# Low parts and sums of squares on VectorE, and a block-wise store of h, in one stage of a hybrid decoder layer

## The chip, the cores and the metric

The kernel runs on one core of a Trainium2 chip. The metric is the device time of one execution in microseconds (us); the figure given is the median of several runs. The engines are called as in the profile: PE is TensorE (its weight loads are shown apart as PEld), DVE is VectorE, ACT is ScalarE, POOL is GpSimd, and SP is the engine whose queue issues nearly all DMA transfers. L702 means line 702 of the kernel before.

## The reference

One inference step of one decoder layer, for a prompt of 1024 tokens and 8 samples of 4 tokens each, 1056 tokens in all, with D = 1024:

```python
h = x + concat([rwkv7(z), pool(z)]) @ w_out        # z = rmsnorm(x) @ w_in
h = h + peer_ffn(rmsnorm(h))                       # product-key experts
h = h + (p @ ple_w) * sigmoid(rmsnorm(h) @ ple_gate_w)
y = rmsnorm(h)

# peer_ffn, for each token and each of 8 heads:
q = xn @ wq                                        # 8 heads x 2 halves x 128
s1, s2 = q[:, :, 0] @ keys[0].T, q[:, :, 1] @ keys[1].T
v1, i1 = top_k(s1, 16); v2, i2 = top_k(s2, 16)     # 128 keys each
sc, ci = top_k(v1[..., :, None] + v2[..., None, :], 16)
gate = softmax(sc)
out = sum_k gelu(u[expert_k] . xn) * gate_k * v[expert_k]
```

The results are the normed outputs and the new states of the recurrence and of the pooling. All of it is float32.

## The kernel before, in words

The hidden states are kept transposed: 128 features on the partitions, 8 blocks of features (KB = 8), and tokens along the free dimension. A product that needs float32 accuracy is made from three products in a faster rounded format (float32r): a matrix x is split into a high part hi, which is x rounded by ACT's copy, and a low part lo = x - hi, and the product is hi*hi + hi*lo + lo*hi (`mm3`, L647 to L656).

The program has these stages. `phase_a` makes the projections and the operands of the recurrence. `bchunk` works through the recurrence in chunks of 64 tokens (`b_stream`). `phase_c(gi)`, the function that the change edits, takes one group of tokens at a time; there are four groups (`GROUPS`): tokens 0 to 288, 288 to 544, 544 to 800 and 800 to 1056. `t_stream(gi)` selects the top experts of a group (`top`, `select`: many short DVE instructions) and writes the gates of the first 672 tokens as dense matrices, for which one-hot products on PE and copies on ACT are used (L901 to L912). The long last stage computes the experts densely for those 672 tokens on PE (L1112), while the remaining 384 tokens are served by gathered rows on POOL and DVE (L1221 to L1238), and then the last gate and norm.

`phase_c(gi)` does the following for its n = 288 or 256 tokens. It loads y, the output of the recurrence, and h, which already holds x and the pooling part of the first product. It splits the four blocks of y into `yhi` and `ylo` (`split`: ACT makes hi, POOL makes lo). For each of the 8 blocks b of h it loads the weights (`wblock`), makes the product (`mm3`), adds it to h (L696, DVE), squares the sum (L698, ACT) and adds the square to `sa` (L700, POOL). Then one DMA stores all 8 blocks of h to the DRAM tensor `hT_d` (L702), from which a later stage reads them. `sa` is summed over the partitions by a product with ones (L704), and `inv_sqrt` makes `rstd` from it (L178: square root on ACT; L179: reciprocal on DVE). L710 then scales each block of h in place on DVE, and `split` makes the high part (L679, ACT) and the low part of it (POOL). These are the operands of 16 more products with `wq`, whose results go through the keys (L739) to the score tensor `sc_d`, from which `top` of that group reads. The weights of groups 1 to 3 come from a stored split copy `wc_d` (L642 and L643, three buffers each); in group 0 they are split and stored on the way (L636 to L640).

The helper `PTT` (L126, L127) issues a tensor_tensor on POOL; `TT` issues one on DVE. In the profile all instructions of `PTT` stand on L127 and are told apart by their tiles: `lo<-y,hi`, `lo<-h,hi`, `sa<-sa,sq`.

What sets the order: `merge` interleaves the streams of one step as they are traced, in the proportion of their lengths. Step 1 runs `phase_c(0)` beside chunks of the recurrence, step 2 `phase_c(1)` beside the selection of group 0 and more chunks, step 3 `phase_c(2)` beside the selection of group 1, and step 4 `phase_c(3)` and the first 8 dense blocks (`upre`), with the selection of group 2 traced ahead of them. A planner then goes over the traced program with estimated costs and writes a fixed order for each engine (`schedule_with_timeline_sim=True`, L1403). On the chip each engine, and SP's queue of DMA issues, follows its written order; an instruction that waits holds back all that stands behind it. The planner also derives the waits from the reads and writes of tiles: L710, which overwrites h, waits for the store that reads it.

The lines that the change touches are L680, L700 and L702.

Of the kernel before, what the change touches and what calls it, by code (L numbers as in the profile page):

```python
# [10 lines left out]
F32 = mybir.dt.float32  # L11
# [5 lines left out]
ALU = mybir.AluOpType  # L17
# [46 lines left out]
def body(ctx, tc, io):  # L64
    nc = tc.nc
    mm = nc.tensor.matmul
    TT, STT, TS, ACT = (nc.vector.tensor_tensor, nc.vector.scalar_tensor_tensor, nc.vector.tensor_scalar,
                        nc.scalar.activation)
# [3 lines left out]
    hT_d = dram.tile([128, KB, T], F32, name="hT_d")  # L72
# [13 lines left out]
    def v3(ap, n):  # L86
        return ap.rearrange("p (a b) -> p a b", b=n)
# [5 lines left out]
    def vec(base, i):  # L93
        return vecs[:, base + i:base + i + 1]
# [31 lines left out]
    def PTT(out, a, b, op):  # L126
        nc.gpsimd.tensor_tensor(out, a, b, op=op)  # L127

    def PS(tag):
        return pools[tag].tile([128, 512], F32, name="ps", tag="bc" if tag in ("b0", "b1") else tag)  # L130
# [46 lines left out]
    def inv_sqrt(out, src, scale, eps):  # L177
        ACT(out, src, AF.Sqrt, bias=eps, scale=scale)  # L178
        nc.vector.reciprocal(out, out)  # L179
# [443 lines left out]
    def wblock(gi, b):  # L623
        if gi == 0 and b % 4 == 0 and b != 4:
            wraws[0] = gp.tile([128, EB, TC], F32, name="gst", bufs=2)
        if b >= C3E and gi == NG - 1:
            hi, lo = esplit(io["wq"][b - KB], PTT)
            return [(t[0], t[1]) for t in zip(*[(x[:, :HK], x[:, HK:]) for x in (hi, lo)])]
        out = []
        for i in range(1 if b < KB else 2):  # L630
            ks = slice(i * HK, (i + 1) * HK)
            hi = ws.tile([128, HK, 128], F32R, name="whi", bufs=3)
            lo = ws.tile([128, HK, 128], F32R, name="wlo", bufs=3)
            if gi == 0:
                raw = v3(wraws[0][:, 16 * (i + b % KB if b < KB else 2 * ((b - KB) % 4) + i):][:, :16].rearrange("p a b -> p (a b)"), 128)
                nc.sync.dma_start(raw, (io["w_out"][b] if b < KB else io["wq"][b - KB])[:, ks, :])  # L636
                ACT(hi, raw, AF.Copy)
                TT(lo, raw, hi.bitcast(F32), op=ALU.subtract)
                nc.sync.dma_start(wc_d[b, :, 0, ks, :], hi.bitcast(F32))
                nc.sync.dma_start(wc_d[b, :, 1, ks, :], lo.bitcast(F32))  # L640
            else:
                nc.sync.dma_start(hi.bitcast(F32), wc_d[b, :, 0, ks, :])  # L642
                nc.sync.dma_start(lo.bitcast(F32), wc_d[b, :, 1, ks, :])  # L643
            out.append((hi, lo))
        return out

    def mm3(ps, w, x, n):  # L647
        xhi, xlo = x
        K = len(w) * HK
        for k in range(K):  # L650
            whi, wlo = w[k // HK]
            kk = k % HK
            mm(ps[:, :n], whi[:, kk, :], xhi[:, k, :n], start=k == 0, stop=False)  # L653
            mm(ps[:, :n], whi[:, kk, :], xlo[:, k, :n], start=False, stop=False)  # L654
            l = mm(ps[:, :n], wlo[:, kk, :], xhi[:, k, :n], start=False, stop=k == K - 1)  # L655
        return l.ins  # L656
# [7 lines left out]
    def segs(gi):  # L664
        c0, c1 = GROUPS[gi]
        if c0 == 0:
            return ((0, NP, NSMP), (NSMP, 0, c1 - NSMP))
        return ((0, c0 - NSMP, c1 - c0),)

    def tiles_of(gi):  # L670
        n = GROUPS[gi][1] - GROUPS[gi][0]
        return [(t, min(128, n - t)) for t in range(0, n, 128)]

    def phase_c(gi):
        c0, c1 = GROUPS[gi]
        n = c1 - c0

        def split(k, src, hi, lo):
            ACT(hi[:, k, :n], src, AF.Copy)  # L679
            PTT(lo[:, k, :n], src, hi[:, k, :n].bitcast(F32), op=ALU.subtract)  # L680

        y = work.tile([128, 4, maxn], F32, name="y", tag="yp")
        nc.sync.dma_start(y[:, :, :n], y_d[:, :, c0:c1])
        h = work.tile([128, KB, maxn], F32, name="h")
        for d, s, L in segs(gi):
            nc.sync.dma_start(h[:, :, d:d + L], hx_d[:, :, s:s + L])
        yhi = mv.tile([128, KB, maxn], F32R, name="hi")
        ylo = mv.tile([128, KB, maxn], F32R, name="lo")
        for k in range(HK):
            split(k, y[:, k, :n], yhi, ylo)  # L690
        sa = work.tile([128, maxn], F32, name="sa")
        for b in range(KB):
            w = wblock(gi, b)
            ps = PS("b2")
            mm3(ps, w, (yhi, ylo), n)
            TT(h[:, b, :n], ps[:, :n], h[:, b, :n], op=ALU.add)  # L696
            sq = work.tile([128, maxn], F32, name="sq", bufs=1) if b else sa
            ACT(sq[:, :n], h[:, b, :n], AF.Square)  # L698
            if b:
                PTT(sa[:, :n], sa[:, :n], sq[:, :n], op=ALU.add)  # L700
            yield
        nc.sync.dma_start(hT_d[:, :, c0:c1], h[:, :, :n])  # L702
        psr = PS("b2")
        mm(psr[:, :n], ones, sa[:, :n], start=True, stop=True)  # L704
        rstd = work.tile([128, maxn], F32, name="rstd", tag="sa")
        inv_sqrt(rstd[:, :n], psr[:, :n], 1.0 / D, eps_t)
        nhi = mv.tile([128, KB, maxn], F32R, name="hi")
        nlo = mv.tile([128, KB, maxn], F32R, name="lo")
        for k in range(KB):
            STT(h[:, k, :n], h[:, k, :n], vec(V_G2, k), rstd[:, :n], op0=ALU.mult, op1=ALU.mult)  # L710
            split(k, h[:, k, :n], nhi, nlo)
        a, b = max(c0, GA), min(c1, GB)
        if a < b:
            for d, t in ((xh_d, nhi), (xl_d, nlo)):
                nc.sync.dma_start(d[:, :, a - GA:b - GA], t[:, :, a - c0:b - c0].bitcast(F32))
        for t0, m in tiles_of(gi):
            pos = c0 + t0
            if GA <= pos < GB:
                continue
            gp = pos - GB  # L720
            for half in range(2):
                ps = PS("b2")
                for k in range(4):
                    nc.tensor.transpose(ps[:m, k * 128:(k + 1) * 128], h[:, half * 4 + k, t0:t0 + m], ident)
                xt = work.tile([128, 512], F32, name="xt", tag="yp")
                ACT(xt[:m], ps[:m], AF.Copy)
                nc.sync.dma_start(xt_d[gp:gp + m, half * 512:half * 512 + 512], xt[:m])
        for j in range(HEADS // 2):
            q = work.tile([128, 4, maxn], F32, name="q", tag="yp")
            for i in range(4):  # L730
                w = wblock(gi, KB + 4 * j + i)
                ps = PS("b2")
                mm3(ps, w, (nhi, nlo), n)
                ACT(q[:, i, :n], ps[:, :n], AF.Copy)
                yield
            for t0, m in tiles_of(gi):
                ps = PS("b2")
                for i in range(4):
                    mm(ps[:m, i * 128:(i + 1) * 128], q[:, i, t0:t0 + m], keys[:, i % 2, :],  # L739
                       start=True, stop=True)  # L740
                st = tk.tile([128, 4, 128], F32, name="scs", bufs=2)
                ACT(st[:m], v3(ps[:m, :], 128), AF.Copy)
                nc.sync.dma_start(sc_d[TIDX[c0 + t0], :m, 4 * j:4 * j + 4, :], st[:m])
# [677 lines left out]
```

## Time and profile before

| | us |
|---|---|
| median of 3 runs | 3302.07 (3301.97 to 3302.18) |
| the profiled execution | 3310.19 |
| its span, first to last instruction | 3308.5 |
| PE busy | 3115.4 (94%) |
| DVE busy | 2561.4 (77%) |
| POOL busy | 1509.4 (46%) |
| ACT busy | 1127.6 (34%) |
| mean granted TensorE clock | 0.968 of full speed |

The profile shows one execution. Times inside it are counted from the first instruction of the span; the rest of the profiled execution's time, 1.7 us, lies around the span. A row of a timeline gives start, length, engine, line and operation, and in brackets how long the engine was idle before and what released it. A row of a group by line gives the shortest, median and longest duration in ns. An instruction's duration may overlap the next one's a little, so the busy time of a group can be less than count times mean.

### The profile page before, as it was taken

The numbers are of one execution on the slowest core, as the hardware profiler recorded it, in microseconds if no ns is written. First come the engines' busy times: TensorE is split into PE (matmuls) and PEld (weight loads), VectorE is DVE, ScalarE is ACT, GpSimd is POOL, SyncE is SP. The second block draws the span as 40 slices with busy tenths as digits, with TensorE's granted clock in tenths as the row PEclk, the third lists the DMA queues.
The fourth block names the chain that finished last, engine by engine and source line by source line (L and its number), as shares of the span: only waits on it lengthen the run. The fifth ranks groups of instructions, "written<-read, shape, count | busy, mean of one in ns | idle before, by whom it ended". The sixth has DMA issues, their size and how long they took to land.

```text
span 3308.5 us, 66279 instructions
## 1 busy us (share of the span) xinstructions
PE 3115.4 (94%) x26777; PEld 2995.7 (91%) x26777; DVE 2561.4 (77%) x4989; ACT 1127.6 (34%) x1734; POOL 1509.4 (46%) x1223
## 2 busy tenths in 40 slices
PE   8998898987888798999999999999999999999997
PEld 7886787877877787999999999999999999999996
DVE  7775333469689688888888888888888888888966
ACT  6442423434554555332222122122222222212243
POOL 5212232222132041146666665666566666666534
PEclk9999999998998898999999999999999999999998
DMA  3325557866875977569999999999999999999834
GB/s 117 117 88 126 156 139 231 277 177 179 241 218 179 296 237 229 198 225 343 336 345 337 327 348 331 327 344 344 330 334 347 331 329 341 337 327 343 316 109 129
DMA packets 437332, 858.88 MB, mean 260 GB/s; under 512 B 108960, under 2 KB 232096, under 8 KB 432544
## 3 DMA queue, kind: packets, MB, share of 16 engines
q1 hardware_dynamic: 326432, 451.93, 42.1%
q0 software_dynamic: 110592, 402.70, 33.6%
q8 instruction: 210, 3.44, 0.4%
q14 instruction: 98, 0.80, 0.1%
HBM read 733.92 MB, written 120.60 MB: 258 GB/s over the span
## 4 chain that ended last, share of the span: by engine, by line
PE 77%; DVE 9%; DMA 8%; ACT 2%; issue 2%; POOL 1%; SPq 1%; ACTq 0%; DVEq 0%; POOLq 0%
PE pd L1112 58%; PE ps L470 5%; PE ps L219 4%; PE ps L653 2%; PE ps L655 2%; PE ps L654 2%; DMA whi<-wc_d 2%; PE ps L909 2%; PE ps L302 1%; DMA scq<-sc_d 1%; DMA sc_d<-scs 1%; DMA wlo<-wc_d 1%; DMA hT_d<-h 1%; PE ps L739 1%; DVE I L762 1%
## 5 line engine op out<-in xcount | busy, mean ns | idle before, releaser
L1221 POOL DMA_INDIRECT row<-u,idx x384 | 546.6, 1423 | 313.8 <-DVE row L1229 134.1
L1221 POOL DMA_INDIRECT row<-v,idx x384 | 536.5, 1397 | 310.8 <-DVE po L1238 142.0
L1088 ACT ACTIVATE ehi<-eraw 128x1024 fp32r<-128x1024 f32 x278 | 294.7, 1060 | 1115.0 <-PE pd L1112 1014.7
L1112 PE MATMUL pd<-XH,elo 128*128 128x336 f32 x2176 | 514.7, 318 | 4.7 <-DVE elo L1090 3.1
L1112 PE MATMUL pd<-XL,ehi 128*128 128x336 f32 x2176 | 515.4, 318 | 0.0
L1112 PE MATMUL pd<-XH,ehi 128*128 128x336 f32 x2176 | 513.4, 317 | 0.3 <-ACT ehi L1088 0.2
L1112 PE MATMUL pd<-wh,ehi 128*128 128x336 f32 (+1 forms) x2112 | 503.4, 317 | 6.5 <-DVE tg L1302 6.5
L1112 PE MATMUL pd<-wh,elo 128*128 128x336 f32 (+1 forms) x2112 | 503.7, 317 | 0.0
L1112 PE MATMUL pd<-wl,ehi 128*128 128x336 f32 (+1 forms) x2112 | 502.3, 317 | 0.0
L1238 DVE SCALAR_TENSOR_TENSOR po<-row,act,po 128x1024 f32<-128x1024 f32 x381 | 488.6, 1283 | 6.7
L1229 DVE SCALAR_TENSOR_TENSOR row<-row,xt 128x1024 f32<-128x1024 f32 x384 | 455.7, 1220 | 9.7 <-DMA row<-u,idx 6.3
L1112 PEld LDWEIGHTS pd<-XH,elo 128*128 128x128 f32 x2176 | 374.1, 189 | 5.7 <-DVE elo L1090 3.5
L1090 DVE TENSOR_TENSOR elo<-eraw,ehi 128x1024 fp32r<-128x1024 f32 x256 | 315.8, 1234 | 79.0 <-ACT ehi L1088 73.2
L1112 PEld LDWEIGHTS pd<-XH,ehi 128*128 128x128 f32 x2176 | 373.3, 189 | 1.1 <-ACT ehi L1088 0.7
L1112 PEld LDWEIGHTS pd<-XL,ehi 128*128 128x128 f32 x2176 | 372.0, 189 | 0.2
L1112 PEld LDWEIGHTS pd<-wh,ehi 128*128 128x128 f32 x2112 | 362.3, 188 | 7.2 <-issue 7.0
L1112 PEld LDWEIGHTS pd<-wl,ehi 128*128 128x128 f32 x2112 | 362.4, 188 | 0.0
L1112 PEld LDWEIGHTS pd<-wh,elo 128*128 128x128 f32 x2112 | 361.7, 188 | 0.2
L653 PE MATMUL ps<-hi,whi 128*128 128x256 f32 (+1 forms) x592 | 189.3, 322 | 48.7 <-DMA whi<-wc_d 21.1
L127 POOL TENSOR_TENSOR ltm<-lts,nmt 128x256 f32<-128x256 f32 x98 | 82.1, 846 | 311.8 <-PE ps L470 189.0
L1181 DVE TENSOR_TENSOR OT<-pd,OT 128x672 f32<-128x672 f32 x120 | 102.9, 858 | 142.8 <-PE pd L1112 142.1
L910 ACT ACTIVATE gst<-ps 128x512 f32<-128x512 f32 x168 | 169.5, 1110 | 67.1 <-PE ps L909 62.0
(426 smaller groups left out, 5256.2 us busy)
## 6 DMA issues: line engine op xcount, KB each, us to landing
eraw<-uT SPq DMA_DIRECT2D x128, 512.0 KB, 6.4
eraw<-vP SPq DMA_DIRECT2D x128, 512.0 KB, 6.4
g_d<-gst SPq DMA_DIRECT2D x21, 2048.0 KB, 9.8
gq<-g_d SPq DMA_DIRECT2D x32, 1344.0 KB, 9.6
whi<-wc_d SPq DMA_DIRECT2D x108, 256.0 KB, 4.9
wlo<-wc_d SPq DMA_DIRECT2D x108, 256.0 KB, 5.2
fdc<-fd SPq DMA_DIRECT2D x16, 896.0 KB, 7.6
wc_d<-whi SPq DMA_DIRECT2D x40, 256.0 KB, 4.6
```

The source lines that it names most:

```text
L127: nc.gpsimd.tensor_tensor(out, a, b, op=op)
L219: mm(ps[:, :XW], s[:, k, :], x[:, k, a:b], start=first, stop=last)
L470: mm(o[hs], l[hs], r[hs], start=start, stop=stop)
L653: mm(ps[:, :n], whi[:, kk, :], xhi[:, k, :n], start=k == 0, stop=False)
L910: ACT(st[:, :, t2 + q:t2 + q + 4].rearrange("p e t -> p t e"), v3(ps, 128), AF.Copy, scale=1.0 / GS)
L1088: ACT(hi, raw, AF.Copy)
L1090: sub(lo, raw, hi.bitcast(F32), op=ALU.subtract)
L1112: mm(ps[:, a, :n], w_[:, k, :], x_[:, s:s + n], start=first, stop=last)
L1181: TT(halves(OT[db]), ps[:, :, :NH], halves(OT[db]), op=ALU.add)
L1221: nc.gpsimd.indirect_dma_start(out=r[:m], out_offset=None, in_=io[tab], in_offset=bass.IndirectOffsetOnAxis(ap=idx[:m, hh, k:k + 1], axis=0))
L1229: STT(r[:m], r[:m], 1.0, xt[:m], op0=ALU.mult, op1=ALU.mult, accum_out=pre[:m, k:k + 1])
L1238: STT(po[:m], r[:m], act[:m, k:k + 1], po[:m], op0=ALU.mult, op1=ALU.add)
```

## The change

In `phase_c`, the low part that `split` makes and the running sum of squares are issued on DVE (`TT`) instead of POOL (`PTT`). The store of h to `hT_d` is issued inside the loop over the blocks, one block at a time, behind the sum of that block's square, instead of once for all 8 blocks after the loop. Nothing else is edited; the values computed are the same.

```diff
         def split(k, src, hi, lo):
             ACT(hi[:, k, :n], src, AF.Copy)
-            PTT(lo[:, k, :n], src, hi[:, k, :n].bitcast(F32), op=ALU.subtract)
+            TT(lo[:, k, :n], src, hi[:, k, :n].bitcast(F32), op=ALU.subtract)
...
             ACT(sq[:, :n], h[:, b, :n], AF.Square)
             if b:
-                PTT(sa[:, :n], sa[:, :n], sq[:, :n], op=ALU.add)
-            yield
-        nc.sync.dma_start(hT_d[:, :, c0:c1], h[:, :, :n])
+                TT(sa[:, :n], sa[:, :n], sq[:, :n], op=ALU.add)
+            nc.sync.dma_start(hT_d[:, b, c0:c1], h[:, b, :n])
+            yield
```

## The prediction

> **What bounds the kernel now.** I read the busy shares and the slices first, then the chain of waits, then windows over the stretch that the edited function fills, then the timeline at the four places where a token group turns from its first product to its second. From the page, the busy row, the slices of PE and DVE, and the engines of the chain:
>
> ```profile
> PE 3115.4 (94%) x26777; PEld 2995.7 (91%) x26777; DVE 2561.4 (77%) x4989; ACT 1127.6 (34%) x1734; POOL 1509.4 (46%) x1223
> PE   8998898987888798999999999999999999999997
> DVE  7775333469689688888888888888888888888966
> PE 77%; DVE 9%; DMA 8%; ACT 2%; issue 2%; POOL 1%; SPq 1%; ACTq 0%; DVEq 0%; POOLq 0%
> ```
>
> A slice is 82.7 us. From the 17th slice on PE never leaves 9; before it PE has 7s and 8s. The windows (columns: length, then busy time of PE, PEld, DVE, ACT, POOL with counts, granted clock, DMA share, GB/s) split this at about 1345 us:
>
> ```profile
> 1345.00:3300.00 1955.00, 1938.67 (x12549) 1934.18 (x12548) 1672.57 (x2373) 520.42 (x639) 1163.82 (x826) 1.00 0.86 308
> 525.00:1340.00 815.00, 693.45 (x8950) 633.45 (x8948) 596.21 (x2235) 388.91 (x679) 192.54 (x233) 0.90 0.76 232
> 705.00:825.00 120.00, 93.52 (x1357) 83.76 (x1353) 113.23 (x542) 49.64 (x99) 36.75 (x52) 0.83 0.59 173
> 945.00:1060.00 115.00, 99.58 (x1456) 88.26 (x1454) 111.46 (x532) 52.52 (x104) 36.70 (x52) 0.87 0.64 191
> 1185.00:1245.00 60.00, 54.08 (x381) 51.93 (x380) 59.72 (x274) 31.83 (x49) 27.75 (x28) 0.94 0.68 209
> ```
>
> After 1345 us PE is busy 1938.7 of 1955 us and none of the edited lines runs there: that stage keeps its length. The change can act only on the 815 us before, where PE is idle 815 - 693.5 = 121.5 us. That is the most that could be won. The last three rows hold the turns of groups 1, 2 and 3. There DVE, which also runs the top-k selection of the group before, is busy 113.2 + 111.5 + 59.7 = 284.4 of 295 us (96%) while PE has 247.2 (84%). In the rest of the 815 us DVE has 311.8 of 520 (60%).
>
> **The turns.** Timeline rows (start, length, engine, line) of groups 0, 1, 2 and 3 in order:
>
> ```profile
> 564.05 0.46 DVE L696 TENSOR_TENSOR h<-ps,h 128x288 f32<-128x288 f32 x1 [0.83 <-PE ps L655]
> 565.62 6.60 SPq L702 DMA_DIRECT2D hT_d<-h  x1
> 567.29 1.95 DVE L179 RECIPROCAL rstd<-rstd 128x288 f32<-128x288 f32 x1 [2.18 <-ACT rstd L178]
> 577.75 2.35 DVE L710 SCALAR_TENSOR_TENSOR h<-h,vecs,rstd 128x288 f32<-128x288 f32 x4 [8.50 <-DMA hT_d<-h]
> 740.81 0.56 SPq L702 DMA_DIRECT2D hT_d<-h  x1
> 756.81 0.47 ACT L178 ACTIVATE rstd<-ps,eps_t 128x256 f32<-128x256 f32 x1
> 763.69 1.74 DVE L179 RECIPROCAL rstd<-rstd 128x256 f32<-128x256 f32 x1
> 767.05 5.63 DVE L710 SCALAR_TENSOR_TENSOR h<-h,vecs,rstd 128x256 f32<-128x256 f32 x8
> 982.64 1.75 DVE L179 RECIPROCAL rstd<-rstd 128x256 f32<-128x256 f32 x1
> 984.57 0.55 SPq L702 DMA_DIRECT2D hT_d<-h  x1
> 993.98 5.61 DVE L710 SCALAR_TENSOR_TENSOR h<-h,vecs,rstd 128x256 f32<-128x256 f32 x8 [2.00 <-DMA hT_d<-h]
> 1224.43 0.47 ACT L178 ACTIVATE rstd<-ps,eps_t 128x256 f32<-128x256 f32 x1
> 1228.52 1.73 DVE L179 RECIPROCAL rstd<-rstd 128x256 f32<-128x256 f32 x1
> 1231.95 5.61 DVE L710 SCALAR_TENSOR_TENSOR h<-h,vecs,rstd 128x256 f32<-128x256 f32 x8
> ```
>
> ```profile
> 566.00:579.00 13.00, 5.06 (x119) 4.44 (x120) 3.21 (x4) 2.18 (x5) 0.78 (x2) 0.84 0.92 242
> 735.00:768.00 33.00, 16.66 (x306) 14.08 (x301) 31.78 (x170) 6.66 (x17) 7.34 (x14) 0.71 0.38 101
> 975.00:996.00 21.00, 15.19 (x281) 12.87 (x279) 18.92 (x99) 10.98 (x25) 5.19 (x9) 0.81 0.79 221
> 1215.00:1234.00 19.00, 13.55 (x80) 12.25 (x78) 19.00 (x70) 9.76 (x17) 6.53 (x5) 0.90 0.61 200
> ```
>
> L710 overwrites h in place, so it has to wait until the one store of the whole h (L702) has read it. In group 0 rstd is ready at 569.24, and L710 starts at 577.75: 8.5 us that DVE spends idle on the store, and PE has only 5.06 of 13 us of work meanwhile. In group 2 rstd is ready at 984.39 and L710 starts at 993.98, with DVE filled by selection work for all but 2.0 us. In groups 1 and 3 no wait for the store shows, but the order on DVE and ACT, written beforehand by the planner, puts other work between: in group 3 rstd's square root ends at 1224.90, its reciprocal comes 3.6 us later. PE's idle time in the four rows is 7.9, 16.3, 5.8 and 5.5 us.
>
> **The change part by part.** The prices:
>
> ```profile
> L127 POOL TENSOR_TENSOR lo<-h,hi x32: 724/906/1179, 578.8 to 1238.8; 128x256 fp32r<-128x256 f32 x24, 128x288 fp32r<-128x288 f32 x8
> L127 POOL TENSOR_TENSOR lo<-y,hi x16: 722/738/1181, 522.9 to 1177.3; 128x256 fp32r<-128x256 f32 x12, 128x288 fp32r<-128x288 f32 x4
> L127 POOL TENSOR_TENSOR sa<-sa,sq x28: 716/740/1332, 541.5 to 1221.3; 128x256 f32<-128x256 f32 x21, 128x288 f32<-128x288 f32 x7
> L696 DVE TENSOR_TENSOR h<-ps,h x32: 398/416/459, 537.0 to 1220.3; 128x256 f32<-128x256 f32 x24, 128x288 f32<-128x288 f32 x8
> L710 DVE SCALAR_TENSOR_TENSOR h<-h,vecs,rstd x32: 458/944/1061, 577.7 to 1236.6; 128x256 f32<-128x256 f32 x24, 128x288 f32<-128x288 f32 x8
> L710 DVE SCALAR_TENSOR_TENSOR h<-h,vecs,rstd 128x256 f32<-128x256 f32 x24 | 16.8, 770 | 2.0 <-DMA hT_d<-h 2.0
> L638 DVE TENSOR_TENSOR wlo<-gst,whi x40: 668/691/1321, 528.3 to 678.1; 128x512 fp32r<-128x512 f32 x40
> ```
>
> *Stores by block.* The wait for one store of 1 MB becomes eight stores of 128 KB, seven of them long issued when rstd is ready. The last is read only by the eighth L710, some 3 us after the first. What is late next is rstd itself (569.24). Group 0: PE's 7.9 us of idle time go, and no other work is queued for DVE there; I take -8 (bounds 0 and -8.5). Groups 1 to 3: the planner no longer has to hold L710 behind the store, but the selection work that now fills DVE has to be done anyway; what PE can win is its idle time, 16.3 + 5.8 + 5.5 = 27.6 us at most, nothing at least. In group 1 the sequence waits behind selection on ACT and DVE as well, and the only store wait that DVE shows there is the 2.0 us of group 2. I take about a third: -10.
>
> *The queue on SP.* 28 DMA issues are added, none removed from the traffic: the same bytes in the same rows. A store of a similar kind and SP's waits:
>
> ```profile
> L1048 SPq DMA_DIRECT2D hx_d<-x x24: 319/327/3133, 421.7 to 516.0; - x24
> hx_d<-x SPq DMA_DIRECT2D x21, 176.0 KB, 2.3
> SPq L642 <- PE ps L655: 114.9, 46, 7.3
> PE ps L653 <- DMA whi<-wc_d: 21.1, 9, 4.9
> ```
>
> 28 x 0.33 = 9 us of SP's time over 815 us, on a queue that already waits 114.9 us for PE to free weight buffers. Each store waits for DVE's h; queued behind it are the weight loads of the next blocks, for which PE waits (21.1 us now). A block's h comes 0.42 us after its last matmul, or later when DVE is full, and the load three blocks ahead needs that same matmul, so the two come due together. I take +1 (bounds 0 and +12, which is half a microsecond for each of 24 stores).
>
> *Low parts and sums on DVE.* 48 low parts and 28 sums, 76 instructions, leave POOL. No row shows DVE doing these with 256 columns and both inputs in SBUF; the nearest are L696 at 0.416 us, same size, and half of L638, 0.35 us: I take 0.416. Groups 1 to 3 have 19 each: 57 x 0.416 = 23.7 us. Back comes what POOL's low parts cost L710 beside them: it takes 0.944 us at the median and 0.458 at best, and POOL's own instruction 0.906 beside it against 0.724. With POOL gone the 24 take 24 x 0.458 = 11.0 instead of 16.8: -5.8. Net +17.9 us of DVE in the stretches that are 96% full. Group 0's share falls where DVE is idle and is covered. Of the 17.9 I put half on the path, +9 (bounds 0 and +17.9): PE and DVE share the chain there, and DVE has gaps later. In the phase itself the low part after the last L710 no longer trails on POOL, and each turn's last sum takes 0.42 for 0.74: -2 (bounds 0 and -6). A new head-of-line wait comes in: a low part on DVE waits for ACT's high part, and behind it stands selection work; with L710 of the next block between, the 0.42 us of the high part are mostly covered. The planner also writes a new order for all that surrounds the edit. No row prices that; it is part of why the range is wide.
>
> The Trainium skill, "SBUF — State Buffer", section "Who interferes with whom", says that a VectorE instruction with two SBUF inputs and a GpSimd instruction that reads SBUF exclude each other for the whole instruction. The trace agrees (0.944 against 0.458 us), so moving the low parts costs DVE less than its 23.7 us; without that rule the sum would be 3 us later.
>
> The Trainium skill, "Perfetto Trace Analysis", section "Identifying the Most-Contended Engine", says to relieve the engine with the highest occupancy. Here that is DVE, at 96%, and the change loads it further; by that rule all of the 17.9 us would count, and the sum would come to -1; rival D below is this case without the gain of the turns.
>
> *Sum.* -8 - 10 + 1 + 9 - 2 = -10 us. The profiled execution took 3310.19 us (span 3308.5 and 1.7 around it), 8.1 above the median of the runs. 3310.2 - 10 = 3300.2 profiled, so 3292 for the median.
>
> **The rivals.** *B, the planner closes all turns:* without the store all of 27.6 us of PE's idle time in groups 1 to 3 goes. -8 - 27.6 + 1 + 9 - 2 = -27.6: 3274. For it speaks the late reciprocal of group 3; against it that DVE is full in these stretches. *C, the gain stays in group 0:* -8 + 0 + 1 + 9 - 1 = +1: 3303. For it: only 2.0 us of store wait show on DVE after group 0. *D, DVE becomes the bound of groups 1 to 3:* the 57 instructions stand in its queue ahead of selection, PE waits for both, and nothing is won by the earlier turn: -8 + 17.9 + 1 = +11: 3313. It decides from the point where more than 8 of the 17.9 us are on the path and the turns do not move. For it: 96%. *E, the stores hold up the weights on SP:* +12 in place of +1, so +1 in all: 3303. *The change does not do what it says:* if the dependence is kept for all of h, the first L710 waits for the eighth store. That lands 2.3 us after its issue by the row above, near 567, before rstd; this moves nothing.
>
> **How the numbers follow.** Forecast 46%, B 16%, C 16%, D 15%, E 7%. The forecast's own range is 3284 to 3299. Cutting half of B below and half of D above leaves 3276 to 3311. A difference under 0.2% (6.6 us) cannot be told from none. Faster: B and four fifths of the forecast, 0.53. Same: the rest of the forecast, most of C and E, 0.28. Slower: D and their remainders, 0.19.
>
> **What would show it.** L710 of group 0 within 1 us of the reciprocal's end, and PE's gap after 570 us gone; L710 at 0.46 us; low parts and sums on DVE near 0.42; DVE's sum over 525 to 1340 up by 15 to 25 us; the dense stage starting about 10 us earlier, at its old length. I am wrong if the turns of groups 1 to 3 stay as long as they are, if PE's waits for weights grow beyond 21 us by more than 5, or if the dense stage changes in length.

## The result, and the profile after

The changed kernel takes 3287.69 us at the median (3280.0 to 3289.57), the kernel before 3302.12 in the same comparison; the ratio is 0.9947 with a 95% interval of 0.9937 to 0.9957, a gain of 17.5 us (14 to 21). A gain in us is worked out from the ratio here and below, and the ratio takes in all runs of both kernels; the two medians alone differ by 14.4 us. The prediction was 3292 in a range of 3276 to 3311, faster: the direction and the range held. The gain is larger than the -10 us of the sum; the experiments ask which terms of the sum are in it.

The profiled execution took 3289.57 us with a span of 3287.9, 20.6 us less than before. From its page, the busy row and the slices of PE and DVE:

```profile
PE 3106.8 (94%) x26777; PEld 2988.9 (91%) x26777; DVE 2583.3 (79%) x5065; ACT 1125.6 (34%) x1734; POOL 1445.6 (44%) x1147
PE   8998898978988798999999999999999999999997
DVE  6775334479689788998888888888888888988966
```

PE ran the same 26,777 products. Its idle time is 3287.9 - 3106.8 = 181.1 us, against 3308.5 - 3115.4 = 193.1 before: 12.0 us less. The other 8.6 us of the 20.6 are busy time: the same products took PE 3106.8 instead of 3115.4 us. The mean granted clock is 0.972 against 0.968. The sum had no term for that: it took PE's idle time as all that could be won.

The dense stage kept its length. The row of its gelu (first and last start at the end of the figures), first before, then after:

```profile
L1118 ACT ACTIVATE wt<-pd x120: 710/715/735, 1364.5 to 3126.3; 128x672 f32<-128x672 f32 x120
```

```profile
L1118 ACT ACTIVATE wt<-pd x120: 709/713/734, 1343.0 to 3104.9; 128x672 f32<-128x672 f32 x120
```

It starts 21.5 us earlier, where about 10 were forecast, and lasts 1761.9 us instead of 1761.8. All of the gain was made before it, as predicted.

The turns of groups 0 to 3 after the change (timeline; start, length):

```profile
566.72 6.03 SPq L701 DMA_DIRECT2D hT_d<-h  x1
566.92 1.95 DVE L179 RECIPROCAL rstd<-rstd 128x288 f32<-128x288 f32 x1 [1.38 <-ACT rstd L178]
568.91 3.09 DVE L710 SCALAR_TENSOR_TENSOR h<-h,vecs,rstd 128x288 f32<-128x288 f32 x7
575.09 0.52 DVE L710 SCALAR_TENSOR_TENSOR h<-h,vecs,rstd 128x288 f32<-128x288 f32 x1 [1.61 <-DMA hT_d<-h]
751.24 0.47 ACT L178 ACTIVATE rstd<-ps,eps_t 128x256 f32<-128x256 f32 x1
754.00 1.73 DVE L179 RECIPROCAL rstd<-rstd 128x256 f32<-128x256 f32 x1
759.50 2.45 DVE L710 SCALAR_TENSOR_TENSOR h<-h,vecs,rstd 128x256 f32<-128x256 f32 x6
974.46 1.75 DVE L179 RECIPROCAL rstd<-rstd 128x256 f32<-128x256 f32 x1
977.15 1.26 DVE L710 SCALAR_TENSOR_TENSOR h<-h,vecs,rstd 128x256 f32<-128x256 f32 x2
1211.29 0.47 ACT L178 ACTIVATE rstd<-ps,eps_t 128x256 f32<-128x256 f32 x1
1214.82 1.74 DVE L179 RECIPROCAL rstd<-rstd 128x256 f32<-128x256 f32 x1
1220.38 2.06 DVE L710 SCALAR_TENSOR_TENSOR h<-h,vecs,rstd 128x256 f32<-128x256 f32 x5
```

Seven blocks of group 0 are scaled right behind the reciprocal, 8.8 us earlier than before. Only the eighth still waits for its own store, 1.6 us, since that store's issue stood late on SP and took 6.03 us. In group 2, L710 starts 0.9 us after rstd (976.21) instead of 9.6. In group 1, it starts 3.8 us after the reciprocal ends (1.6 before) and 29.2 us after the last sum of h (730.26; before 740.37 and 26.7 us); in group 3, 3.8 us after the reciprocal ends, where it was 1.7, and 16.5 us after the last sum of h, where it was 11.6. From the last sum of h to L710 the turns of groups 1 to 3 take 29.2 + 7.3 + 16.5 = 53.0 us, against 26.7 + 15.7 + 11.6 = 54.0 before: group 2 gains what groups 1 and 3 lose. The windows of the four turns and of the whole stretch (columns as in the prediction):

```profile
566.00:579.00 13.00, 10.57 (x130) 9.07 (x129) 9.88 (x20) 6.26 (x15) 0.00 (x0) 0.87 0.82 220
726.00:758.00 32.00, 16.78 (x310) 14.57 (x308) 31.43 (x148) 7.01 (x17) 9.00 (x13) 0.72 0.31 79
967.00:988.00 21.00, 16.85 (x298) 14.36 (x297) 21.00 (x115) 10.80 (x26) 2.93 (x4) 0.92 0.80 231
1198.00:1222.00 24.00, 18.05 (x112) 16.40 (x110) 24.00 (x90) 9.71 (x17) 5.44 (x3) 0.91 0.35 110
525.00:1340.00 815.00, 701.72 (x9050) 643.70 (x9049) 632.94 (x2350) 395.53 (x691) 136.46 (x160) 0.91 0.77 237
```

PE idles 2.4 us at the turn of group 0 (7.9 before), 15.2 at that of group 1 (16.3), 4.2 at that of group 2 (5.8) and 6.0 at that of group 3 (5.5; that window is 24 us long now and was 19). The long gap at group 1 stayed.

The same rows show where the lead over the kernel before arises. At the first L710 of groups 0 to 3 it is 8.8, 7.6, 16.8 and 11.6 us, and at the first gelu of the dense stage 21.5 us. So the lead of group 0's turn is still there 190 us later, and more than half of the gain is made behind group 1's turn.

The moved instructions, and two rows of waits over 525 to 1340 us (total, times, longest):

```profile
L680 DVE TENSOR_TENSOR lo<-h,hi x32: 396/414/454, 571.9 to 1227.5; 128x256 fp32r<-128x256 f32 x24, 128x288 fp32r<-128x288 f32 x8
L680 DVE TENSOR_TENSOR lo<-y,hi x16: 402/420/458, 522.8 to 1160.6; 128x256 fp32r<-128x256 f32 x12, 128x288 fp32r<-128x288 f32 x4
L700 DVE TENSOR_TENSOR sa<-sa,sq x28: 397/418/2425, 541.0 to 1206.0; 128x256 f32<-128x256 f32 x21, 128x288 f32<-128x288 f32 x7
L710 DVE SCALAR_TENSOR_TENSOR h<-h,vecs,rstd x32: 427/475/946, 568.9 to 1223.7; 128x256 f32<-128x256 f32 x24, 128x288 f32<-128x288 f32 x8
SPq L642 <- PE ps L655: 93.4, 46, 7.0
PE ps L653 <- DMA whi<-wc_d: 26.9, 10, 4.6
```

The low parts take 0.414 to 0.420 us on DVE, and L710 fell from 0.944 to 0.475 us. DVE's busy time over the whole span rose by 2583.3 - 2561.4 = 21.9 us. The eighth store's issue began at 566.72, and the eighth L710, which it released, came at 575.09, 8.4 us later; the prediction had it landed 2.3 us after its issue.

### The profile page after: what moved, and what is told of

Same layout as the page of the kernel before. It is cut to its first block, busy times and chain, and to the rows that moved or that the text cites. A ratio compares the mean times of both kernels' runs of the same rounds, so it can differ in the third digit from the quotient of the medians.

```text
span 3287.9 us, 66335 instructions
## 1 busy us (share of the span) xinstructions
PE 3106.8 (94%) x26777; PEld 2988.9 (91%) x26777; DVE 2583.3 (79%) x5065; ACT 1125.6 (34%) x1734; POOL 1445.6 (44%) x1147
## 4 chain that ended last, share of the span: by engine, by line
PE 69%; DVE 8%; DMA 4%; ACT 1%; issue 0%; SPq 0%; POOL 0%; ACTq 0%; DVEq 0%; POOLq 0%
PE pd L1112 59%; PE ps L470 2%; PE ps L909 2%; PE ps L653 2%; PE ps L655 2%; PE ps L654 1%; DMA whi<-wc_d 1%; DMA scq<-sc_d 1%; PE ps L739 1%; DVE ab L901 1%; DMA wlo<-wc_d 1%; DMA sc_d<-scs 1%; DVE I L762 0%; ACT gst L910 0%; DVE V L761 0%
## 5 line engine op out<-in xcount | busy, mean ns | idle before, releaser
L653 PE MATMUL ps<-hi,whi 128*128 128x256 f32 (+1 forms) x592 | 189.5, 321 | 48.5 <-DMA whi<-wc_d 26.9
L655 PE MATMUL ps<-hi,wlo 128*128 128x256 f32 (+1 forms) x592 | 185.2, 313 | 5.0 <-DMA wlo<-wc_d 4.3
```

## The experiments

Every ratio below is against the kernel before on the same chip; kernels that ran on different chips are compared by these ratios. Most of these edits also make the planner write another order, which the later experiments look at by itself. "The turn" is the place between the last sum of h and the first product with `wq`.

**One part alone: the store by blocks.**

```diff
-            yield
-        nc.sync.dma_start(hT_d[:, :, c0:c1], h[:, :, :n])
+            nc.sync.dma_start(hT_d[:, b, c0:c1], h[:, b, :n])
+            yield
```

> Only the store by blocks; low parts and sums stay on POOL. Theory S (the store makes the gain: about 9 us at the turn of group 0 and 9 at that of group 2, and the moved instructions are about neutral): -14 to -20 us, first L710 of group 0 near 569 us. Theory M (the move to DVE makes more than half of the gain): -5 to -9 us, group 0's turn alone. Theory P (the gain behind group 0 is an accident of the planner's order): -8 us from group 0, and the rest anywhere between -10 and +10.

Measured: 3280.19 against 3302.46 us, ratio 0.9935 (0.9914 to 0.9956), -21 us. This kernel gains as much as the full change: its time cannot be told from that of the full change (the intervals overlap). Theory M falls.

**The other part alone: the move to DVE.**

```diff
-            PTT(lo[:, k, :n], src, hi[:, k, :n].bitcast(F32), op=ALU.subtract)
+            TT(lo[:, k, :n], src, hi[:, k, :n].bitcast(F32), op=ALU.subtract)
...
-                PTT(sa[:, :n], sa[:, :n], sq[:, :n], op=ALU.add)
+                TT(sa[:, :n], sa[:, :n], sq[:, :n], op=ALU.add)
```

> Only the move to DVE; one store of the whole h as before. Theory S: between -3 and +6 us, the first L710 of group 0 still at about 578 us and that of group 2 still some 10 us after rstd. Theory M: -10 us or better with the waits for the store still there. Theory P: no number of its own, but the turns of groups 1 to 3 move by several us either way.

Measured: ratio 1.0005 (0.9992 to 1.0017), +1.6 us (-3 to +6): no change. The wait in group 0 is as before; in the timeline of this kernel:

```profile
569.99 1.95 DVE L179 RECIPROCAL rstd<-rstd 128x288 f32<-128x288 f32 x1 [1.38 <-ACT rstd L178]
579.73 2.66 DVE L710 SCALAR_TENSOR_TENSOR h<-h,vecs,rstd 128x288 f32<-128x288 f32 x6 [7.79 <-DMA hT_d<-h]
```

**Low parts and store, sums left on POOL.**

```diff
-                TT(sa[:, :n], sa[:, :n], sq[:, :n], op=ALU.add)
+                PTT(sa[:, :n], sa[:, :n], sq[:, :n], op=ALU.add)
```

The diff is against the changed kernel.

> Low parts on DVE and the store by blocks; the sums of squares stay on POOL. Theory S: within 3 us of the full change (-14 to -21 us), since 28 sums of 0.42 us are little. Theory M: the low parts are what counts, so the same as the full change. Theory P: off the full change by more than 5 us, with no cause in the sums themselves.

Measured: ratio 0.9946 (0.9926 to 0.9966), -18 us. Where the sums are made does not show.

**The store by blocks in group 0 alone, and in groups 1 to 3 alone.** Both against the changed kernel:

```diff
+            if gi == 0:
                 nc.sync.dma_start(hT_d[:, b, c0:c1], h[:, b, :n])
             yield
+        if gi:
+            nc.sync.dma_start(hT_d[:, :, c0:c1], h[:, :, :n])
```

> The full move to DVE, but the store by blocks in group 0 alone; groups 1 to 3 keep the one store. Theory S: the gain of group 0 (8 to 9 us) without that of group 2: -6 to -11 us, and L710 of group 2 again about 10 us after rstd. Theory M: -17 us, as the full change. Theory P: group 0 as in the full change, the rest anywhere.

Measured: ratio 0.9952 (0.9935 to 0.9970), -16 us. Stores by block in group 0 alone give what the full change gives, although in this kernel L710 of group 2 waits again (980.9 us, rstd at 973.9). The number is that of theory M, but the move alone gave nothing. The shorter turn of group 2 shows nothing in the whole time here.

The second kernel has the two conditions exchanged.

> The full change, but group 0 keeps the one store. Theory W: group 0's turn waits again (first L710 near 578 us) and the gain is nearly gone, 0 to -5 us, although group 2's turn is shorter. The prediction's third of the idle time of groups 1 to 3: -8 to -12 us.

Measured: ratio 0.9986 (0.9975 to 0.9997), -4.6 us, with L710 of group 0 at 580.0 us. Against the move alone (1.0005) that is -6 us, give or take as much. The turn of group 2 did not become shorter in this kernel, as had been expected: its square root of rstd comes late on ACT (992.50 us), and L710 starts 24.7 us after the last sum of h, where it was 15.7 before and 7.3 in the full change. So this kernel does not show what a shorter turn of group 2 is worth.

**The wait taken away without smaller stores.** The kernel before, in which group 0 writes the scaled blocks into another tile:

```diff
+            if gi == 0 and k % 4 == 0:
+                hn = work.tile([128, 4, maxn], F32, name="hn", tag="yp")
+            hs = h[:, k, :n] if gi else hn[:, k % 4, :n]
-            STT(h[:, k, :n], h[:, k, :n], vec(V_G2, k), rstd[:, :n], op0=ALU.mult, op1=ALU.mult)
-            split(k, h[:, k, :n], nhi, nlo)
+            STT(hs, h[:, k, :n], vec(V_G2, k), rstd[:, :n], op0=ALU.mult, op1=ALU.mult)
+            split(k, hs, nhi, nlo)
```

> The kernel before, with one store of the whole h and the moved instructions on POOL; in group 0 alone the scaled block goes into another tile, so that nothing waits for the store. Theory W (the wait of group 0's L710 on the store is the cause, however the store is cut): the first L710 of group 0 at about 569 to 571 us, and -12 to -18 us in all, as the store by blocks in group 0 gave. Theory B (the smaller stores themselves help, by what they do to the queues): 0 to -6 us.

Measured: ratio 0.9949 (0.9932 to 0.9967), -17 us, with one store of the whole h and all moved instructions on POOL. In its timeline and on its page:

```profile
569.69 1.95 DVE L179 RECIPROCAL rstd<-rstd 128x288 f32<-128x288 f32 x1 [2.18 <-ACT rstd L178]
571.68 2.35 DVE L713 SCALAR_TENSOR_TENSOR hn<-h,vecs,rstd 128x288 f32<-128x288 f32 x4
PE 3099.6 (94%) x26777; PEld 2981.5 (91%) x26777; DVE 2564.2 (78%) x4989; ACT 1126.8 (34%) x1734; POOL 1504.5 (46%) x1223
```

The first scaled block follows the reciprocal at once. At this place it counts that group 0 does not wait for the store, not how the store is cut. PE's busy time is 15.8 us below that of before, for the same products. Theory W fits all kernels up to here: those without that wait are 16 to 21 us faster, those with it -4.6 to +1.6. It fits no longer when the order alone is changed, below.

**More work on DVE.** The changed kernel with each low part computed twice, which leaves the result as it is:

```diff
             TT(lo[:, k, :n], src, hi[:, k, :n].bitcast(F32), op=ALU.subtract)
+            TT(lo[:, k, :n], src, hi[:, k, :n].bitcast(F32), op=ALU.subtract)
```

> The full change with every low part computed twice on DVE: 48 instructions of 0.42 us more, 36 of them in groups 1 to 3 (15 us). The prediction's half on the path: +7 us against the full change (-10 us against before). If DVE sets the end of groups 1 to 3: +15 (-2 against before). If DVE's time is covered there: within 4 us of the full change (-14 to -20).

Measured: ratio 1.0038 (1.0024 to 1.0053), +12.6 us against before and some 30 against the full change. That is outside all three expectations, and more than the added instructions last. From its page and its groups:

```profile
L681 DVE TENSOR_TENSOR lo<-h,hi x32: 402/412/449, 579.9 to 1261.8; 128x256 fp32r<-128x256 f32 x24, 128x288 fp32r<-128x288 f32 x8
L681 DVE TENSOR_TENSOR lo<-y,hi x16: 410/416/939, 526.3 to 1183.9; 128x256 fp32r<-128x256 f32 x12, 128x288 fp32r<-128x288 f32 x4
PE 3127.8 (94%) x26777; PEld 3006.2 (90%) x26777; DVE 2592.7 (78%) x5113; ACT 1125.2 (34%) x1734; POOL 1447.6 (43%) x1147
```

48 x 0.414 us are 20 us, and the span of 3327.8 is 39.9 longer than that of the changed kernel: 21.0 us more of PE's busy time and 18.9 more of idle time (3327.8 - 3127.8 = 200.0). A price of DVE's time alone cannot give this; the order differs too. The profiled execution took 3329.56 us, 9.7 above the median of this kernel.

**The order alone.** The kernel before with the same work, interleaved otherwise:

```diff
-    CL = [0, 24, 24, 24, 24]
+    CL = [0, 25, 25, 25, 25]
```

> The kernel before with the same work; the function of the groups is taken as 25 steps long instead of 24 where the streams are interleaved, so that only the order differs. Theory P (the planner's order alone moves the time by several us): 5 us or more either way. Theories W and B: within 4 us of before.

Measured: ratio 0.9951 (0.9932 to 0.9969), -16 us, and L710 of group 0 still waits 4.85 us for the store (8.50 before; it starts at 574.05, 3.7 us earlier). And with 23 steps:

> The kernel before in a third order, with 23 steps. Theory P: again several us away from before, so that with 24 and 25 steps three orders show how far the order alone moves the time. If the order of before is simply a poor one: -8 to -16 us here too. If 25 steps were a lucky hit: within 4 us.

Measured: ratio 0.9917 (0.9897 to 0.9936), -27 us, with the store's wait in group 0 still there (5.7 us of DVE's idle time). This is faster than the changed kernel, without any of the change. At group 0's first L710 it is 2.6 us behind the kernel before (580.31), at those of groups 1, 2 and 3 it is 18.9, 22.0 and 37.6 us ahead. The first large step is the turn of group 1; its rows, and the row of the kernel before on which the comparison rests:

```profile
739.70 0.48 ACT L178 ACTIVATE rstd<-ps,eps_t 128x256 f32<-128x256 f32 x1
743.71 1.74 DVE L179 RECIPROCAL rstd<-rstd 128x256 f32<-128x256 f32 x1
748.17 5.62 DVE L710 SCALAR_TENSOR_TENSOR h<-h,vecs,rstd 128x256 f32<-128x256 f32 x8
731.00:752.00 21.00, 15.62 (x298) 13.84 (x296) 21.00 (x61) 7.91 (x19) 9.17 (x11) 0.83 0.54 141
```

```profile
753.86 0.70 ACT L775 ACTIVATE F<-I 128x128 f32<-128x128 uint32 x2 [10.52 <-DVE I L766]
```

The last sum of h starts at 732.46 in this kernel, and L710 15.7 us later; before it was 26.7 us later (740.37 to 767.05), with PE idle 16.3 of 33 us. In both kernels the square root is made on ACT and waits there in its written place. Here that place is ahead of the copies of the selection's indices (L775); before it was behind them, and ACT stood idle for 10.52 us until DVE had found these indices. The other 18.7 us of the lead at group 3 arise behind this turn; what makes them stays open. Theory P holds in this: the order alone moves the time by as much as the whole change.

**The change in another order.** The changed kernel, and the store by blocks alone, both with 25 steps as above.

> The full change, interleaved with the function of the groups taken as 25 steps long; the kernel before gained 16 us by that alone. Theory A (the change's gain and that of the order add up): -28 to -35 us. Theory P (both come to the same thing, a better order behind group 0): -14 to -22 us, so that the change is worth no more than 6 us in this order.

> Only the store by blocks, interleaved as with 25 steps: the candidate for a kernel faster than both. Theory A: -32 to -40 us. Theory P: -16 to -25 us.

Measured: ratio 0.9919 (0.9896 to 0.9942), -27 us, and 0.9917 (0.9899 to 0.9935), -27 us. Against the kernel before with the same 25 steps (0.9951) the change gains 0.0032, 10.6 us, with an uncertainty of about 10 (half-widths 0.0023 and 0.0018 combined). The wait that the change takes away in this order is 4.85 us long, not 8.50. The gain lies between both theories, and the numbers do not exclude either end. These two kernels and the third order of before are the fastest that were measured, at 3275 to 3276 us, and cannot be told apart.

**PE kept busy through the wait.** The kernel before with 48 products whose result nobody reads:

```diff
+        if gi == 0:
+            pw = PS("b2")
+            for i in range(48):
+                mm(pw[:, :n], yhi[:, 0, :128], yhi[:, 1, :n], start=True, stop=True)
         rstd = work.tile([128, maxn], F32, name="rstd", tag="sa")
```

> The kernel before with 48 products more on PE in group 0, between the sum of squares and the scaled blocks, whose results nobody reads: PE works through the wait for the store. To be read from the stretch behind the wait, not from the whole time. If PE's idle time is what halves the granted clock there: no half-speed stretch near 585 us, and the first products after the wait follow one another in 0.13 us instead of 0.24 us. If not: half speed as before.

Measured in one execution: the windows behind the wait, first of the kernel before, then of this one:

```profile
572.00:580.00 8.00, 1.21 (x6) 0.93 (x8) 2.25 (x4) 1.48 (x4) 1.18 (x2) 0.68 0.64 212
580.00:590.00 10.00, 10.00 (x63) 8.60 (x60) 7.58 (x10) 4.57 (x10) 6.86 (x8) 0.75 0.46 159
```

```profile
572.00:580.00 8.00, 5.08 (x67) 4.47 (x67) 3.03 (x5) 1.69 (x4) 1.90 (x3) 0.99 0.52 185
580.00:590.00 10.00, 10.00 (x70) 7.69 (x70) 6.88 (x9) 4.41 (x10) 6.10 (x7) 0.84 0.54 191
```

With PE at work the granted clock stays at 0.99 through the wait and falls to 0.84 after it, where 2.9 us of idle time are left; with PE idle it is 0.68 and then 0.75, although PE is busy all of the 10 us. The stretch at half clock (granted clock 0.50) is 10.2 us long in the kernel before, from 574.9 on, and 3.4 us here, from 579.8 on. Part of the expectation held: the stretch is shorter, but it did not vanish.

That alone would put the half clock down to the wait. The kernel with the store by blocks alone, the first experiment, speaks against it. There the first seven L710 do not wait and PE has only 1.16 us of idle time before the first product with `wq`, and yet the same windows show a low clock:

```profile
570.67 5.27 DVE L710 SCALAR_TENSOR_TENSOR h<-h,vecs,rstd 128x288 f32<-128x288 f32 x7
571.72 0.40 PE L653 MATMUL ps<-hi,whi 128*128 128x288 f32 x1 [1.16 <-ACT hi L679]
572.00:580.00 8.00, 7.95 (x42) 6.25 (x42) 6.12 (x8) 3.75 (x9) 6.92 (x8) 0.60 0.67 161
580.00:590.00 10.00, 10.00 (x86) 9.27 (x85) 2.41 (x4) 2.63 (x6) 0.73 (x1) 0.80 1.01 315
```

Its half clock lasts from 573.7 to 583.9, as long as before; the same kernel with 25 steps has 1.00 in both windows. So taking the wait away does not by itself take the half clock away, and what sets it here stays open. The execution with the added products took 3283.3 us, 20 less than before with more work on PE: its order differs as well, and the time says nothing on the clock.

## Why the prediction was right or wrong, point by point

**What bounds the kernel.** Right as to the place: the dense stage kept its length to 0.1 us over 120 gelus, and the gain arose before it. That is so for these two kernels; in the experiments the row of the 120 gelus lasts 1761 to 1772 us, and the move alone began it 9.3 us earlier than before (1355.2) and ended it at the same 3126.3. Wrong was that PE's idle time, 121.5 us, is the most that could be won: up to the first gelu of the dense stage the change took 12.1 us of idle time and 9.4 us of busy time from PE. The reading that PE never leaves 9 from the 17th slice on leaves out the last slice, a 7; no sum uses it.

**Stores by block, group 0: -8.** Right in mechanism and size at its place: L710 8.8 us earlier, the first product behind it about 9 (the end of the first `wq` product's copy moved from 588.5 to 579.1 us). The kernel with another tile shows that the wait is what held L710. About half of the gain of 17.5 us stands at this place, and the lead is still 7.6 us at group 1's first L710.

**Groups 1 to 3: -10.** The size was wrong, and so was the place. L710 of group 2 follows rstd 8.7 us sooner, as hoped, and the whole turn is 8.4 us shorter, yet the kernel with stores by block in group 0 alone is as fast (0.9952 against 0.9947). The turns of groups 1 and 3 grew by 2.5 and 4.9 us, so that the three together are only 1.0 us shorter. "The turns of groups 1 to 3 stay as long as they are" was a sign of error that the prediction had set, and in their sum it came true. Stores in groups 1 to 3 alone gave -4.6 us together with the move, or about -6 against the move, but there the turn of group 2 was not shorter. The third of PE's idle time that I took was a guess from a bound, not a chain of waits. The biggest gap, at group 1, has another cause, which the prediction named and did not price: rstd's square root stands behind selection work on ACT, which waits 10.52 us for DVE.

**SP: +1.** No cost of the stores shows. PE's waits for weights grew from 21.1 to 26.9 us, which is past the 5 us that I had set as a sign of error; but with the stores alone they are 21.0, and with the move alone 29.9. The growth goes with the move or its order, not with the 28 issues. The eighth store of group 0 came later than forecast and held its own block for 1.6 us.

**DVE: +9, and -2 for the shorter trail.** The prices of single instructions were right: 0.414 to 0.420 us where 0.416 was taken, L710 at 0.475 for 0.458, and 21.9 us more of DVE's time over the whole span, where 17.9 for groups 1 to 3 and 19 x 0.416 = 7.9 for group 0 make 25.8 at most. (Over 525 to 1340 us the rows show +36.7, more than the 15 to 25 forecast, because in the changed kernel that window takes in more of the dense stage. From 525 us to the first gelu of that stage DVE has 635.94 us instead of 615.75, +20.2.) The share on the path was oversized as far as the runs show: the move alone costs 1.6 us (-3 to +6), not 7. The full change against the store alone is +4, and the same pair with 25 steps +1; neither is clear of noise, and the order differs in each pair too. Rival D, 17.9 us on the path, does not show. The rule that the prediction set beside this, of the Trainium skill, "Perfetto Trace Analysis", section "Identifying the Most-Contended Engine", is to optimize first the engine with the highest occupancy. It did not decide here: DVE was the fullest engine of these stretches and took more work at no measured cost. The kernel with doubled low parts lost 30 us, but its order is not the same, and how much of that is DVE's time stays open.

**The sum.** -10 was the total of a right term, an oversized gain, a cost that does not show and two terms that were missing. One is PE's busy time, 8.6 of the 20.6 us between the two profiled executions, on the same products. It goes with a higher granted clock (0.89 before and 0.91 after over 690 to 1345 us, 0.94 and 0.95 over 525 to 690), so most of it does not lie at group 0's wait; why the clock is higher is not shown. The other is the planner's order. That the time came near the forecast is partly luck, and the range held because it reached across.

**What no term and no rival had: the planner's order.** The prediction said that no row prices it and widened the range. Two reorderings with no change of work gave -16 and -27 us, and the order the kernel had before is the slowest of three. How much of the 17.5 us comes from the missing wait (about 9 us are seen at its place) and how much from the new order behind it is not settled: in the one other order where both kernels were run the change is worth 10.6 us, give or take 10.

## What to carry to other kernels

Where a planner writes the order, time the unchanged work in two or three orders before crediting a change of half a percent to its edit; a gain that shows at its own place in the timeline (here 9 us at one wait) is the part to trust. An overwrite in place behind a large store is a wait that a block-wise store, or another tile, takes away. PE's busy time is no fixed quantity: a bound made from its idle time alone left out 8.6 us here.

## What the runs showed of the hardware

Idle time and the granted clock: PE fully busy from 580 to 590 us ran at 0.75 after 6.8 us of idle time in the 8 us before, and at 0.84 after 2.9 us of it. In the kernel with the store by blocks alone it ran at 0.80 after 0.05 us of idle time in those 8 us, and its stretch at half clock was as long (573.7 to 583.9). So the idle time just before does not tell the clock here. Over whole executions the busy time of the same 26,777 products lay between 3099.6 us (mean granted clock 0.974) and 3127.8 us (0.963), a spread of 28 us or 0.9%.

A VectorE instruction beside GpSimd work: L710 takes 0.475 us at the median in the full change and 0.478 with the move alone, where the low parts are on DVE; it takes 0.944 us before and 0.946 with the store alone, where they are on POOL.
